# A never-entered branch with idle instructions at the head of three engine programs

## The chip, the cores and the metric
The kernel runs on one core of one Trainium2 chip. The metric is the device time of one execution in microseconds (us). Three runs of the kernel before gave 166.06, 166.07 and 166.12 us, a median of 166.07 us.

## The reference
The input is `x` with shape (32, 512, 1024) in float32, all values positive, 64 MiB in all. The output is one sum for each row of 1024 values.

```python
def reference(x: np.ndarray) -> np.ndarray:
    return np.sum(1.0 / x, axis=-1).astype(np.float32)
```

So each of the 16384 rows is inverted element by element and summed.

## The kernel before
The 16384 rows lie on 128 partitions, 128 rows on each. A unit of work is one row on every partition, a 128x1024 tile of 512 KB. There are 127 whole units, and the last row is cut into two pieces of 512 columns. Units are loaded into a ring of 46 rows in on-chip memory (`ring`), and their sums are collected in `sums`, 128x128.

Nothing is scheduled by the framework. The string `PLAN` (lines 41 to 59) lists the steps by hand, and the loop at line 161 sends each token to its engine in that order. The letters that matter here are these.

- `D` loads units through SyncE's (SP's) queue, line 170. The first loads are 2, 12, 12, 9 and 11 units; the last ones are single units and the two halves. A load into ring rows that are in use waits for the engines that still read them.
- `A` on ScalarE (ACT), line 178, replaces a unit by the reciprocal of its square root. Squared and summed, that gives the sum of reciprocals.
- `Z` on ACT, line 187, squares and sums in one pass. In the trace each `Z` is two instructions, an ACTIVATE and a read of the accumulator.
- `G` on GpSimd (POOL), line 280, squares; `T` on VectorE (DVE), line 283, sums what POOL squared; `Q` on DVE, line 240, squares and sums at once; `B` on DVE, line 255, takes statistics from which squares are summed later (`K`, `M`).
- For the pair units, `P` on POOL (line 194) multiplies the two halves of a row, `U` on TensorE (PE, line 201) adds the halves, `L` and `E` on ACT (line 211) take the reciprocal square root of the product and square it, and `R` on DVE (line 220) multiplies and sums.
- Stores of parts of `sums` go through SP, line 156: six of them late in the plan and the last one at the end.

At the head, line 70 loads ACT's function table, and `make_identity` at line 90 has POOL fill a 128x128 identity matrix (masks.py:197 and 199) that PE needs for `U`. Ahead of the plan's loop, lines 159 and 160 issue 13 instructions on POOL that do nothing (`EARLY = 13`, line 21). Each engine has a program of its own, a straight line of instructions from head to end; it meets the others only at semaphores. As built, ACT's program for this kernel has 133 instructions (156 with the second half of each `Z` or accumulating step), DVE's 174, POOL's 101, SP's 68 and PE's 48 before its matrix instructions are split. An instruction is 64 bytes long.

Of the kernel before, what the change touches and what calls it, by code (L numbers as in the profile page):

```python
# [11 lines left out]
def kernel(  # L12
# [5 lines left out]
    nc = tc.nc  # L18
    f32 = mybir.dt.float32
    P = 128  # L20
    EARLY = 13
    D = 1024
    H = D // 2
    F = 128
# [67 lines left out]
    def parse(tok):  # L92
        body, _, b = tok[1:].partition("@")
        r, _, n = body.partition("+")
        return tok[0], int(r), int(n or 1), int(b or 0)
# [58 lines left out]
    def store(lo, hi):  # L154
        a, at = divmod(lo, HALF)
        nc.sync.dma_start(out=out_v[a, :, at : at + hi - lo], in_=sums[:, lo:hi])

    with tc.manual_schedule():
        for _ in range(EARLY):
            nc.gpsimd.nop(hint="idle", nofuse=True)  # L160
        for op, u, n, b in (parse(tok) for tok in PLAN):
            if op == "D":
                n, u = u, loaded
                while n:
# [10 lines left out]
                    u, n = u + m, n - m  # L175
# [83 lines left out]
            elif op in "KM":  # L259
                lo, step, n = STATS[u]  # L260
                i = stat_rows.index(lo)
                part = stats[:, i : i + n]
                if op == "K":
# [4 lines left out]
                    engine = "ACT"  # L268
                else:
# [6 lines left out]
                    engine = "DVE"  # L276
# [47 lines left out]
```

## Time and profile before
| what | value |
|---|---|
| median of three runs | 166.07 us (166.06 to 166.12) |
| span of the profiled execution | 164.2 us |
| ACT busy | 145.7 us, 89% of the span |
| DVE busy | 115.9 us, 71% |
| POOL busy | 108.8 us, 66% |
| PE busy | 38.2 us, 23% |
| read from HBM | 67.11 MB, 409 GB/s over the span |
| packets of the queue of data | 4608, 96.3% of 16 DMA engines' span |
| packets of the queue of instructions | 3 |

The profiled execution's own span is 164.2 us, from the first to the last instruction of the program on the core; the runs' times also hold about 1.8 us that lie outside of it. Times inside the span are counted from its start. Busy time does not count instructions that only wait, branch or set registers. The data of a load is cut into one packet per partition and load, and the 16 DMA engines carry the packets side by side. A load has landed when the last of the 16 has brought its part.

### The profile page before, as it was taken

The page shows a single profiled execution, that of the slowest core. Times are in us where ns is not written, and L with a number is a line of the kernel's source. Part 1 is how long each engine was busy: PE and PEld are TensorE (multiplying, and loading weights), DVE is VectorE, ACT ScalarE, POOL GpSimd, SP SyncE. Part 2 cuts the span into 40 slices and gives each one's busy share as a digit, 9 for nine tenths or more (in the row PEclk, how much of TensorE's full clock was granted, in tenths as well). Part 3 has the DMA queues.
Part 4 walks back from the last instruction along what each step waited for, and adds up shares of the span by engine and source line. Part 5 has one row for each costly group of instructions (what it writes and reads, how often), then busy time and mean ns, then how long its engine had stood idle before and what let it go on. Part 6 is the DMA issues. An engine that isn't in the chain of part 4 may idle for free.

```text
span 164.2 us, 640 instructions
## 1 busy us (share of the span) xinstructions
PE 38.2 (23%) x68; PEld 14.4 (9%) x68; DVE 115.9 (71%) x147; ACT 145.7 (89%) x148; POOL 108.8 (66%) x56
## 2 busy tenths in 40 slices
PE   0000000000000000053000000065908198699700
PEld 0000000000000000020000000032302033234200
DVE  0000003559927039999999999999698969999894
ACT  3600199999999999999999999999999999999994
POOL 1000069998999999999507979999926195477300
PEclk9999999999999999999999999999975859999985
DMA  5999899899989899999998998999999999999970
GB/s 188 463 539 407 383 395 563 383 431 431 463 351 527 351 479 409 391 455 431 391 503 383 431 463 381 455 407 441 419 425 467 414 419 422 421 411 417 408 249 2
DMA packets 4611, 67.20 MB, mean 409 GB/s; under 512 B 1408, under 2 KB 1408, under 8 KB 2176
## 3 DMA queue, kind: packets, MB, share of 16 engines
q1 hardware_dynamic: 4608, 67.18, 96.3%
q14 instruction: 3, 0.02, 0.0%
HBM read 67.11 MB, written 0.07 MB: 409 GB/s over the span
## 4 chain that ended last, share of the span: by engine, by line
ACT 63%; DMA 26%; DVE 6%; issue 2%; POOL 2%; SPq 0%; DVEq 0%; POOLq 0%
ACT ring L178 47%; DMA ring<-in_x_dram 26%; ACT ring L187 10%; ACT prod L211 6%; DVE ring L240 2%; DVE stats L255 2%; POOL prod L194 2%; DVE prod L220 1%; DVE sums L283 0%; SPq L170 0%; ACT stats L265 0%; DVE sums L240 0%; DVE sums L220 0%; DVEq L240 0%; POOLq L194 0%
## 5 line engine op out<-in xcount | busy, mean ns | idle before, releaser
L178 ACT ACTIVATE ring<-ring 128x1024 f32<-128x1024 f32 (+4 forms) x65 | 104.1, 1658 | 15.2 <-DMA ring<-in_x_dram 15.1
L280 POOL TENSOR_TENSOR ring<-ring 128x1024 f32<-128x1024 f32 (+2 forms) x33 | 85.9, 2634 | 29.9 <-ACT ring L178 29.9
L283 DVE TENSOR_REDUCE sums<-ring 128x1 f32<-128x1024 f32 (+4 forms) x27 | 53.3, 1999 | 42.2 <-POOL ring L280 42.1
L201 PE MATMUL ps<-ring,ident 128*128 128x512 f32 x68 | 38.2, 712 | 117.2 <-DMA ring<-in_x_dram 115.9
L255 DVE BATCH_NORM_STATS2 stats<-ring 128x6 f32<-128x512 f32 x58 | 36.5, 679 | 3.1 <-ACT ring L178 3.1
L194 POOL TENSOR_TENSOR prod<-ring 128x512 f32<-128x512 f32 x17 | 22.5, 1339 | 15.0 <-DMA ring<-in_x_dram 10.8
L201 PEld LDWEIGHTS ps<-ring,ident 128*128 128x128 f32 x68 | 14.4, 224 | 140.2 <-POOL ring L280 71.6
L187 ACT ACTIVATE ring<-ring 128x1024 f32<-128x1024 f32 x23 | 23.9, 1041 | 0.0
L211 ACT ACTIVATE prod<-prod 128x512 f32<-128x512 f32 x34 | 19.8, 615 | 0.2
L240 DVE CUSTOM_DVE_ANT_0 ring<-ring 128x1024 f32<-128x1024 f32 (+1 forms) x12 | 17.6, 1480 | 0.5 <-ACT ring L178 0.4
L220 DVE CUSTOM_DVE_ANT_0 prod<-prod,ps 128x512 f32<-128x512 f32 x17 | 11.1, 676 | 0.1
L187 ACT ACTIVATION_READ_ACCUMULATOR ring<-ring 128x1 f32 x23 | 4.3, 187 | 0.0
L70 ACT ACT_TABLE_LOAD x1 | 1.3, 1283 | 0.7 <-PEq L308 0.7
L220 DVE DVE_READ_ACCUMULATOR2_ANT sums<- 128x1 f32 x17 | 1.4, 81 | 0.0
L240 DVE DVE_READ_ACCUMULATOR2_ANT sums<- 128x1 f32 x13 | 1.0, 81 | 0.0
L240 DVE CUSTOM_DVE_ANT_0 ring<-ring,sums 128x512 f32<-128x512 f32 x1 | 0.8, 752 | 0.1
masks.py:199 POOL TENSOR_SCALAR_AFFINE_SELECT ident<-ident 128x128 f32<-128x128 f32 x1 | 0.3, 293 | 0.5 <-POOL ident masks.py:197 0.5
L265 ACT ACTIVATE stats<-stats 128x44 f32<-128x44 f32 (+1 forms) x2 | 0.5, 272 | 0.0
L270 DVE TENSOR_REDUCE sums<-stats 128x11 f32<-128x88 f32 (+1 forms) x2 | 0.5, 264 | 0.0
masks.py:197 POOL MEMSET ident<- 128x128 f32 x1 | 0.2, 205 | 0.3 <-POOLq L308 0.3
L308 POOL MEMSET const-float32-0.0<- 128x1 f32 x1 | 0.1, 99 | 0.2 <-issue 0.2
L308 POOL MEMSET const-bfloat16-1.0<- 128x1 bf16 x1 | 0.1, 102 | 0.0
(2 smaller groups left out, 0.2 us busy)
## 6 DMA issues: line engine op xcount, KB each, us to landing
ring<-in_x_dram SPq DMA_DIRECT2D x2, 6144.0 KB, 25.8
ring<-in_x_dram SPq DMA_DIRECT2D x3, 4096.0 KB, 26.0
ring<-in_x_dram SPq DMA_DIRECT2D x3, 3072.0 KB, 26.3
ring<-in_x_dram SPq DMA_DIRECT2D x1, 5632.0 KB, 55.9
ring<-in_x_dram SPq DMA_DIRECT2D x1, 5120.0 KB, 32.4
ring<-in_x_dram SPq DMA_DIRECT2D x1, 4608.0 KB, 43.3
ring<-in_x_dram SPq DMA_DIRECT2D x4, 1024.0 KB, 37.8
ring<-in_x_dram SPq DMA_DIRECT2D x1, 3584.0 KB, 24.4
```

Of the source, the lines that this page charges most:

```text
L70: nc.scalar.add_instruction(mybir.InstLoadActFuncSet(name=nc.get_next_instruction_name(), act_func_set_id=act_sets.index("abs_reciprocal_s ...
L178: inst = nc.scalar.activation(out=area(u, n), in_=area(u, n), func=Arsqrt if op == "A" else Square, scale=FIT if op == "A" else 1.0,)
L187: inst = nc.scalar.activation(out=area(u), in_=area(u), func=Square, accum_out=sums[:, r : r + 1])
L194: inst = nc.gpsimd.tensor_tensor(out=prod[:, b], in0=ring[:, r, :H], in1=ring[:, r, H:], op=mult)
L201: inst = nc.tensor.matmul(ps[:, b], lhsT=ident, rhs=ring[:, r, h * H : (h + 1) * H], start=h == 0, stop=h == 1,)
L211: inst = nc.scalar.activation(out=pair, in_=pair, func=Arsqrt if op == "L" else Square, scale=S * FIT if op == "L" else 1.0,)
L220: inst = nc.vector.tensor_tensor_reduce(out=pair, in0=pair, in1=ps[:, bank[u]], scale=S, scalar=0.0, op0=mult, op1=add, accum_out=sums[:, ...
L240: inst = nc.vector.tensor_tensor_reduce(out=row, in0=row, in1=row, scale=1.0, scalar=total if r in summed else 0.0, op0=mult, op1=add, acc ...
L255: inst = nc.vector.bn_stats(out=stats[:, i, h], in_=ring[:, u % R, h * H : (h + 1) * H])
L265: inst = nc.scalar.activation(out=mean, in_=mean, func=Square, scale=float(H // 2) ** 0.5)
L280: inst = nc.gpsimd.tensor_tensor(out=row, in0=row, in1=row, op=mult)
L283: inst = nc.vector.tensor_reduce(out=sums[:, u : u + n], in_=area(u, n), axis=mybir.AxisListType.X, op=add,)
```

## The change
Lines 159 and 160 go, and with them POOL's 13 idle instructions. In their place, ahead of the plan, a register is set to zero on ACT, DVE and POOL, and a branch compares it with zero. The body of the branch, which is never entered, holds 60 idle instructions on POOL, 44 on ACT and 48 on DVE. Everything else of the program stands as it was.

```diff
-    EARLY = 13
+    EARLY = ((nc.gpsimd, 60), (nc.scalar, 44), (nc.vector, 48))
...
+    skippers = [mybir.EngineType.Activation, mybir.EngineType.DVE, mybir.EngineType.Pool]
+    never = nc.alloc_registers("never", engines=skippers)
+    nc.regs_mov(never, 0)
+    with tc.If(nc.snap(never, engines=skippers) != 0):
+        for engine, n in EARLY:
+            for _ in range(n):
+                engine.nop(hint="idle", nofuse=True)
     with tc.manual_schedule():
-        for _ in range(EARLY):
-            nc.gpsimd.nop(hint="idle", nofuse=True)
         for op, u, n, b in (parse(tok) for tok in PLAN):
```

As built, each of the three programs gains two register moves, the compare-and-branch, the idle instructions and one unconditional branch behind them. That is 48 instructions more ahead of ACT's first ACTIVATE and 52 more ahead of DVE's first reduction. POOL's identity now stands ahead of the branch, and with a repeated one-instruction configuration behind the branch and the 13 idle ones gone its first TENSOR_TENSOR stands 52 further down. SP and PE get one unconditional branch each, to the instruction that follows; SP's stands between the first load and the second. All waits, semaphore counts and tiles of the other instructions are the same in both programs.

## The prediction
> **What bounds the kernel now.** I read the page's busy times and queues first.
>
> ```profile
> span 164.2 us, 640 instructions
> ...
> PE 38.2 (23%) x68; PEld 14.4 (9%) x68; DVE 115.9 (71%) x147; ACT 145.7 (89%) x148; POOL 108.8 (66%) x56
> ...
> q1 hardware_dynamic: 4608, 67.18, 96.3%
> q14 instruction: 3, 0.02, 0.0%
> ```
>
> Two things are nearly full: ACT (145.7 of 164.2 us) and the 16 DMA engines (96.3%). The last row is small but decides this case: three packets of 0.02 MB in all, about 8 KB each, brought instructions while the kernel ran. Next, ACT alone: its first instructions by time, and its busy time in stretches (the columns behind the stretch are its length and ACT's busy time).
>
> ```profile
> 0.74 1.28 ACT L70 ACT_TABLE_LOAD   x1 [0.74 <-PEq L308]
> 5.48 1.91 ACT L178 ACTIVATE ring<-ring 128x2048 f32<-128x2048 f32 x1 [3.46 <-DMA ring<-in_x_dram]
> ...
> 19.97 2.00 ACT L178 ACTIVATE ring<-ring 128x1024 f32<-128x1024 f32 x2 [11.40 <-DMA ring<-in_x_dram]
> ```
> ```profile
> 19.96:100.45 80.49, 80.48 (x66) 1.00 0.99 429
> 100.45:100.67 0.22, 0.00 (x0) 1.00 0.71 223
> 100.67:123.78 23.11, 23.10 (x26) 0.95 1.00 429
> 123.78:123.88 0.10, 0.00 (x0) 0.50 0.00 0
> 123.88:161.90 38.02, 37.82 (x52) 0.86 0.93 383
> ```
>
> ACT waits 11.40 us for the second load, starts at 19.97, and is then busy to 161.90 with two holes, at 100.45 (0.22 us) and 123.78 (0.10 us). At both its next step is the first use of a load. Back-to-back ACT steps overlap by about 0.10 us, so the holes cost about 0.32 and 0.20, together **0.52 us**. So the end is set by when the second load lands, by ACT's 142 us behind it, and by any load that lands late.
>
> **Where the instruction packets fall.** The DMA view, cut to three short windows, finds one packet in each: 65.5 to 66.0, 99.9 to 100.3, and 111.9 to 112.2 us.
>
> ```profile
> q14 instruction: 1, 0.01, 3.9%
> ```
> ```profile
> q14 instruction: 1, 0.01, 5.1%
> ```
> ```profile
> q14 instruction: 1, 0.01, 6.4%
> ```
>
> The share is of 16 engines in the window: 3.9% of 16 x 0.5 us is 0.31 us; the others give 0.33 and 0.31. The data packet behind it suffers as well. At 64.2 to 64.4 seven packets of 40 KB start; at 66.0 to 66.5, behind the first instruction packet, one starts.
>
> ```profile
> q1 hardware_dynamic: 7, 0.29, 331.7%
> ```
> ```profile
> q1 hardware_dynamic: 1, 0.04, 23.7%
> ```
>
> The seven took 331.7% of 3.2 us, 1.52 us each; the one took 23.7% of 8 us, 1.90 us. So one instruction packet sets one DMA engine back by up to 0.31 + 0.38 = **0.69 us**, and since a load lands with its slowest engine, every later load lands later by about that. Holes of 0.32 and 0.20 us at first uses, behind the first packet and behind all three, fit this.
>
> Whose packets are they? 8 KB at 64 bytes is 128 instructions. ACT's program (156) and DVE's (174) are longer than that, so each must pass an 8 KB border at least once. Counted by stretch (PE, PEld, DVE, ACT, POOL in this order):
>
> ```profile
> 0.00:65.80 65.80, 0.00 (x0) 0.00 (x0) 23.96 (x10) 50.17 (x42) 43.79 (x22) 1.00 0.99 424
> 65.80:100.20 34.40, 3.75 (x4) 1.17 (x4) 34.17 (x38) 34.40 (x28) 26.50 (x11) 1.00 0.98 422
> 100.20:112.10 11.90, 4.02 (x6) 1.89 (x7) 11.79 (x13) 11.67 (x11) 11.90 (x6) 1.00 1.01 430
> 112.10:146.00 33.90, 21.43 (x40) 7.74 (x38) 30.78 (x55) 33.70 (x47) 20.30 (x15) 0.85 1.00 427
> 146.00:164.20 18.20, 9.04 (x20) 3.58 (x20) 15.24 (x35) 15.79 (x25) 6.33 (x5) 0.85 0.73 285
> ```
>
> ACT has started 42 instructions at 65.8, DVE 48 at 100.2, POOL 39 at 112.1 (to which its 13 idle ones and some ten that only wait are to be added). The skipped stretch covers ACT's places 7 to 51, DVE's 6 to 54 and POOL's 17 to 77, so I take the first packet as ACT's, the second as DVE's, the third as POOL's: all three borders then lie inside the skipped stretch. ACT has no idle time at 65.8, so the packet is read ahead, not awaited.
>
> **The change, part by part.**
>
> ```profile
> 0.73 0.20 POOL masks.py:197 MEMSET ident<- 128x128 f32 x1 [0.29 <-POOLq L308]
> 1.45 0.29 POOL masks.py:199 TENSOR_SCALAR_AFFINE_SELECT ident<-ident 128x128 f32<-128x128 f32 x1 [0.51 <-POOL ident masks.py:197]
> 22.05 10.57 POOL L280 TENSOR_TENSOR ring<-ring 128x3072 f32<-128x3072 f32 x2 [20.31 <-ACT ring L178]
> ```
> ```profile
> 0.74 2.54 SPq L170 DMA_DIRECT2D ring<-in_x_dram  x5
> ```
> ```profile
> 27.39 3.41 DVE L283 TENSOR_REDUCE sums<-ring 128x1 f32<-128x1024 f32 x2 [27.39 <-POOL ring L280]
> ```
>
> *POOL's 13 idle instructions* lie between 0.73 and 1.45, so they are worth at most 0.72 us, and POOL waits from then to 22.05: gain nothing. *Two moves and the branch* on three engines aren't in this trace. Above, they cannot cost much more than that 0.72 us for 13 idle instructions and more; below, nothing. ACT waits till 5.48, POOL till 22.05, DVE till 27.39, so both ends give 0. Without that cover ACT would pay up to 0.72. *SP's extra branch* delays the second of five issues, which come every 0.5 us and are done at 3.28, while the first load runs till 5.48: 0. [...]
>
> *The three packets* move to the head: entering the next block at about 1 us asks for the one behind it. What follows has four terms.
>
> (a) The 0.52 us of holes can go, since at 100.45 and 123.78 no engine has been set back in mid-run.
>
> (b) At the head the packets may meet the first data. No data packet starts before 1.75 us, and the stretches there (the last columns are the DMA share and GB/s) show:
>
> ```profile
> 1.00:1.75 0.75, 0.00 (x0) 0.00 (x0) 0.00 (x0) 0.75 (x1) 0.29 (x1) 1.00 0.00 0
> 1.75:2.25 0.50, 0.00 (x0) 0.00 (x0) 0.00 (x0) 0.27 (x1) 0.00 (x0) 1.00 1.56 262
> 2.25:4.50 2.25, 0.00 (x0) 0.00 (x0) 0.00 (x0) 0.00 (x0) 0.00 (x0) 1.00 0.90 353
> ```
>
> From SP's first issue (0.74) to the first data is 1.0 us; an instruction packet asked for at 1 us and as slow would come at about 2.0, on top of the first rows. If quicker it is done before them. So the setback is between 0 and 0.69 us, and it moves the second load's landing and ACT's start at 19.97. I take 0.2: it is asked for hardly later than the data, and the engines run below their later rate in that stretch anyway (353 against 429 GB/s), so part of it hides. By 123.9 ACT is ahead by 0.52 - 0.2 = 0.32 us.
>
> (c) The shift brings new borders into the run. ACT's next one is 128 places on, and 48 places come earlier: its instruction 42 + 128 - 48 = 122, 26 from the end. DVE's is 76 instructions behind its 48th, about 124 less the dozen places that only wait, some 35 from the end. By the last row above (x35, x25) both are at about 146 us. POOL has none. So two of the three packets come again, in the tail, and if they use the same DMA engines as before the last loads land as late as now, plus (b).
>
> (d) In the tail the loads are barely ahead of ACT. The load issued at 109.78 and the last one, issued at 148.39, each with its size and us to landing, then ACT's steps that use them:
>
> ```profile
> 109.78 0.33 SPq L170 DMA_DIRECT2D ring<-in_x_dram  x1
> ```
> ```profile
> ring<-in_x_dram SPq DMA_DIRECT2D x1, 1024.0 KB, 38.5
> ```
> ```profile
> 148.39 0.33 SPq L170 DMA_DIRECT2D ring<-in_x_dram  x1
> ```
> ```profile
> ring<-in_x_dram SPq DMA_DIRECT2D x1, 256.0 KB, 11.5
> ```
> ```profile
> 148.56 1.04 ACT L178 ACTIVATE ring<-ring 128x1024 f32<-128x1024 f32 x1
> ```
> ```profile
> 158.74 2.08 ACT L178 ACTIVATE ring<-ring 128x1024 f32<-128x1024 f32 x3
> ```
>
> They land at 148.3 and 159.9; ACT uses them at 148.56 and, as the third of three (0.95 + 0.52 behind 158.74), at 160.2. So ACT can be at most about 0.25 us earlier there before it waits again.
>
> The sum: ACT's gain of 0.32 is cut in the tail to 0.25 - 0.2 = **0.05 us**. The profiled span is 164.24 us and would become 164.2; the runs' median is 1.83 us above it, so 166.07 - 0.05 gives 166.0.
>
> **The rivals.** *Faster: the packets come early and the tail stays free.* If they are done before 1.75 us, (b) is 0; if the tail's packets are absent or fall on engines that have slack, (d) doesn't bind, and the whole 0.52 us is won: 165.55. For it: no data runs before 1.75. Against it: the 8 KB packets, which put the next border at 146. [...]
>
> *Slower: head collision.* If all 0.69 us of (b) is paid, (c) and (d) leave 0.25 - 0.69 = -0.44: 166.5. It decides from 0.58 us on (0.25 + 0.33). For it: three engines are hit, and the slowest counts. Against it: the slow first rows that hide a part.
>
> *Slower: the jump breaks reading ahead.* If a taken branch doesn't start the read of the block behind, ACT and DVE must wait at 146 us for a packet: 1.0 us from asking to the first data, as SP's at the head, plus 0.31, less little: ACT is on the path there, so +1.2: 167.3. [...] Nothing in this trace shows a long jump.
>
> *It doesn't do what it says.* If the borders lie elsewhere, packets only move to other times: 166.05.
>
> **How the numbers follow.** A measurement of this kernel tells about 0.2%, 0.33 us, from no change. Forecast (165.75 to 166.4) 0.49; faster rival 0.25; head collision 0.12; broken reading 0.10; no effect 0.04. Faster 0.25, same 0.49 + 0.04 = 0.53, slower 0.22. The range goes from the faster rival to the collision with a little beyond, 165.5 to 166.6; left out are the broken reading and the edges.
>
> **What would show it.** Right: no instruction packet between 5 and 140 us, none or three near 1 to 2 us, two near 146; the hole at 100.45 gone; ACT's long run starting at 20.0 to 20.3. The faster rival shows ACT starting at 19.97 and no packet in the tail. The collision shows ACT starting at 20.4 or later. Broken reading shows an ACT hole of about 1 us near 146 with no data load as its releaser. Packets in mid-run would make the mapping wrong.

## The result and the profile after
The changed kernel takes 166.81 us (166.75 to 166.99, three runs) against 166.07 us. The ratio is 1.0044, 95% interval 1.0024 to 1.0064: slower by 0.74 us, beyond the predicted range. The profiled execution's span went from 164.2 to 165.0 us. First the page of the changed kernel: span, busy times, queues and the chain that ended last by engine.

```profile
span 165.0 us, 638 instructions
...
PE 39.7 (24%) x68; PEld 14.8 (9%) x68; DVE 116.1 (70%) x147; ACT 145.8 (88%) x148; POOL 108.7 (66%) x56
...
q1 hardware_dynamic: 4608, 67.18, 95.8%
q14 instruction: 5, 0.04, 0.1%
...
ACT 64%; DMA 31%; DVE 2%; issue 1%; SPq 0%; DVEq 0%
```

ACT has the same work (145.8 against 145.7 us). The instruction queue has five packets in the span instead of three, and the chain of waits spends 31% on data loads where it spent 26%. The DMA view cut to four short windows of the changed kernel shows where the five lie: 5.0 to 5.2, 6.6 to 6.8, 149.5 to 149.8 and 151.9 to 152.1 us.

```profile
q14 instruction: 1, 0.01, 9.7%
```
```profile
q14 instruction: 2, 0.02, 19.3%
```
```profile
q14 instruction: 1, 0.01, 6.5%
```
```profile
q14 instruction: 1, 0.01, 10.2%
```

Between 7 and 149 us there are none. What the three at the head cost shows in the data packets that start where they end, at 5.38, 6.98 and 7.02 us. The first line is a data packet of the same size at 6.58 that follows no instruction packet, the other three are these; the windows are 20, 15, 15 and 12 ns long.

```profile
q1 hardware_dynamic: 1, 0.05, 567.2%
```
```profile
q1 hardware_dynamic: 1, 0.05, 849.6%
```
```profile
q1 hardware_dynamic: 1, 0.05, 942.1%
```
```profile
q1 hardware_dynamic: 1, 0.05, 1232.3%
```

The undisturbed packet took 567.2% of 16 x 0.02 us, which is 1.82 us; in the same way the three took 2.04, 2.26 and 2.37. Now ACT by time and, below, by stretches (length, busy time and count, granted clock, DMA share, GB/s):

```profile
5.60 1.91 ACT L183 ACTIVATE ring<-ring 128x2048 f32<-128x2048 f32 x1 [3.58 <-DMA ring<-in_x_dram]
...
20.77 2.00 ACT L183 ACTIVATE ring<-ring 128x1024 f32<-128x1024 f32 x2 [12.08 <-DMA ring<-in_x_dram]
```
```profile
20.76:100.90 80.14, 80.13 (x65) 0.86 1.00 431
100.90:124.10 23.20, 23.20 (x28) 0.72 1.00 429
124.10:154.17 30.07, 30.01 (x43) 0.79 1.00 424
154.17:154.35 0.18, 0.01 (x2) 1.00 1.04 410
154.35:155.40 1.05, 1.05 (x1) 1.00 1.02 406
155.40:155.63 0.23, 0.01 (x2) 1.00 1.08 427
155.63:162.70 7.07, 7.01 (x10) 0.83 0.51 173
```
```profile
154.35 1.06 ACT L183 ACTIVATE ring<-ring 128x1024 f32<-128x1024 f32 x1 [0.17 <-DMA ring<-in_x_dram]
155.63 1.06 ACT L183 ACTIVATE ring<-ring 128x1024 f32<-128x1024 f32 x1 [0.22 <-DMA ring<-in_x_dram]
```

The reader is to see three things. ACT starts its long run 0.80 us later (20.77 against 19.97). Both holes of before, at 100.45 and 123.78, are gone. New holes stand in the tail, at first uses of loads. Matched instruction by instruction in the two traces, ACT is late by 0.80 us from 20 to 100 us, by 0.46 at 102, 0.23 at 124, 0.07 at 150.3, and then by about 0.78 from 155 to the end. So the late start was won back almost wholly, and the tail lost it again. Had the first been all, the time would have been nearly that of before.

The last load, in SP's row and the DMA view of the changed kernel:

```profile
148.46 0.33 SPq L175 DMA_DIRECT2D ring<-in_x_dram  x1
```
```profile
ring<-in_x_dram SPq DMA_DIRECT2D x1, 256.0 KB, 12.3
```

It lands at 160.8 us, 0.9 later than before (148.39 + 11.5); the loads that land behind 153 us are all 0.9 to 1.0 us later.

### The profile page after: what moved, and what is told of

Read it like the earlier page. It is cut to its first block, busy times and chain, and to the rows that moved or that the text cites. A ratio compares the mean times of both kernels' runs of the same rounds, so it can differ in the third digit from the quotient of the medians.

```text
span 165.0 us, 638 instructions
## 1 busy us (share of the span) xinstructions
PE 39.7 (24%) x68; PEld 14.8 (9%) x68; DVE 116.1 (70%) x147; ACT 145.8 (88%) x148; POOL 108.7 (66%) x56
## 4 chain that ended last, share of the span: by engine, by line
ACT 64%; DMA 31%; DVE 2%; issue 1%; SPq 0%; DVEq 0%
ACT ring L183 48%; DMA ring<-in_x_dram 31%; ACT ring L192 13%; ACT prod L216 3%; DVE ring L245 2%; DVE prod L225 0%; SPq L175 0%; ACT stats L270 0%; DVE sums L245 0%; DVEq L245 0%; DVEq L324 0%; DVE sums L225 0%
## 5 line engine op out<-in xcount | busy, mean ns | idle before, releaser
L206 PE MATMUL ps<-ring,ident 128*128 128x512 f32 x68 | 39.7, 735 | 116.7 <-DMA ring<-in_x_dram 115.3
```

Of the source, the lines that this page charges most:

```text
L206: inst = nc.tensor.matmul(ps[:, b], lhsT=ident, rhs=ring[:, r, h * H : (h + 1) * H], start=h == 0, stop=h == 1,)
```

## The experiments
All were compared with the kernel before on the same chip, where its median was 166.06 to 166.08 us. The first question is whether it is the branch or the packets.

**e1, the branch without a shift.**
```diff
-    EARLY = ((nc.gpsimd, 60), (nc.scalar, 44), (nc.vector, 48))
+    EARLY = ((nc.gpsimd, 8), (nc.scalar, 1), (nc.vector, 1))
```


> The same branch on the three engines, but with a body of 1 idle instruction on ScalarE and VectorE and 8 on GpSimd, so that the places of the instructions move by 5, 5 and 0 only and the three instruction packets stay in mid-run. Theory A (the time is lost by instruction packets that meet the load stream at the head and again in the tail): packets near 60, 95 and 112 us, none before 20 us and none behind 140 us, ScalarE starts its second load at 19.9 to 20.1 us, time 166.0 to 166.2. Rival B (the branch, its register moves or the second configuration of GpSimd cost it): ScalarE's start or the end moves by 0.7 us, time 166.7 to 166.9.

Measured: 166.10 us, ratio 1.0003 (0.9994 to 1.0011). The packets came at 64, 93 and 112 us. Branch, register moves and POOL's repeated configuration cost nothing that can be seen. Rival B falls.

**e2, the shift without a branch.**
```diff
-    EARLY = 13
+    EARLY = ((nc.gpsimd, 65), (nc.scalar, 48), (nc.vector, 52))
...
-        for _ in range(EARLY):
-            nc.gpsimd.nop(hint="idle", nofuse=True)
+        for engine, n in EARLY:
+            for _ in range(n):
+                engine.nop(hint="idle", nofuse=True)
```


> No branch: the idle instructions are run at the head, 48 on ScalarE, 52 on VectorE and 65 on GpSimd, so that every later instruction has the same place as in the changed kernel. Theory A: packets at 5 to 10 us and two near 150 us as in the changed kernel, ScalarE's second start at 20.5 to 20.9 us, time 166.6 to 167.0. Rival B: no branch, so 166.0 to 166.2.

Measured: 166.80 us, ratio 1.0046 (1.0033 to 1.0059), packets at 6.6, 6.7, 8.4, 149.0 and 151.8 us, ACT's second start at 20.66. So the places of the instructions decide, not how the idle ones are passed, and rival B falls here too.

**e3, the same shift in mid-run.** It tells the head from the tail.
```diff
+        idle = {"A40+4": (nc.scalar, 48), "T33+3": (nc.vector, 52), "G30+3": (nc.gpsimd, 52)}
+        last = ""
-        for op, u, n, b in (parse(tok) for tok in PLAN):
+        for tok in PLAN:
+            if last in idle:
+                engine, many = idle[last]
+                for _ in range(many):
+                    engine.nop(hint="idle", nofuse=True)
+            last = tok
+            op, u, n, b = parse(tok)
```


> No branch: 48, 52 and 52 idle instructions are run on ScalarE, VectorE and GpSimd near 40 to 55 us, behind long steps; GpSimd keeps its 13 at the head. The first packets then come near 40 to 55 us, the second two near 150 us, none at the head. Theory A1 (the tail's second packets on engines already set back decide the end): ScalarE's second start stays at 19.9 to 20.1 us, a wait of 0.3 to 1 us comes near 100 us, the last loads land 0.5 to 1.0 us later than before, time 166.4 to 166.9. Rival A2 (the late start at the head decides, the tail does nothing): time 166.0 to 166.2.

Measured: 166.73 us, ratio 1.0048 (1.0035 to 1.0061). Two of e3's rows of ACT by time, its second start and the tail:

```profile
20.01 4.66 ACT L186 ACTIVATE ring<-ring 128x1024 f32<-128x1024 f32 x3 [11.40 <-DMA ring<-in_x_dram]
```
```profile
155.51 1.06 ACT L186 ACTIVATE ring<-ring 128x1024 f32<-128x1024 f32 x1 [0.23 <-DMA ring<-in_x_dram]
```

The start is where it was before, and the time is nearly that of the change. The late start is not needed; A2 falls. The second packets came at 148.9 and 151.8 us, as expected. One expectation missed: the first packets came at 59, 64 and 75 us, since ScalarE's and VectorE's idle instructions ran at 59 to 61 and 69 to 72 us, later than I had read from the plan, and no longer wait came at 100 us.

**e4, e5, e6, one engine at a time** (the same branch, on one engine's list; e5 and e6 keep the 13 idle instructions).
```diff
+    EARLY = ((nc.gpsimd, 60),)
+    skippers = [mybir.EngineType.Pool]
```


> The branch and its 60 idle instructions on GpSimd alone; ScalarE's and VectorE's programs keep their places. Theory A1: one packet at 5 to 7 us, two in mid-run at 65 and 100 us, none in the tail; ScalarE's second start is 0.3 to 0.8 us later, and the tail lands as before (each DMA engine is hit once), so time 165.9 to 166.3. Rival A2 (the late start at the head decides): 166.4 to 166.8.

> The branch and its 44 idle instructions on ScalarE alone; GpSimd keeps its 13 run ones, VectorE's program keeps its places. ScalarE's packets: one at 3 to 7 us, one at 149 to 150 us; VectorE's at 100 and GpSimd's at 112 us stay. Theory A1 (setbacks add up on the DMA engine that carries one program's packets, and the slowest engine's total by the tail decides): ScalarE's engine is hit twice, about 0.7 + 0.7 us, so the last loads land 0.3 to 0.6 us later than before and 166.2 to 166.6. Theory A3 (each packet only counts where it falls, nothing adds up): 166.0 to 166.15.

> The branch and its 48 idle instructions on VectorE alone; GpSimd keeps its 13 run ones, ScalarE's program keeps its places. VectorE's packets: one at 3 to 7 us, one at 151 to 152 us; ScalarE's at 65 and GpSimd's at 112 us stay. VectorE's packet cost its DMA engine the most in the kernel before (0.33 + 0.66 us), so by theory A1 the last loads land 0.6 to 1.0 us later than before and the time is that of the whole change, 166.5 to 166.9. Theory A3: 166.0 to 166.15.

Measured: e4 166.09 us, ratio 0.9999 (0.9990 to 1.0008), although ACT started at 20.43; e5 166.41, ratio 1.0014 (1.0004 to 1.0023); e6 166.80, ratio 1.0042 (1.0028 to 1.0055). Each engine's packets moved and the others' stayed, which also names them: ACT's is the one near 66 us, DVE's at 100, POOL's at 112. (One time missed: POOL's packet in e4 came at 3.4 us, not at 5 to 7.) POOL's move is free: e4 has no packet behind 100.5 us, since POOL's program ends before a second border. DVE's alone costs as much as the whole change; in e6 ACT meets the same two waits in the tail.

```profile
154.65 1.06 ACT L185 ACTIVATE ring<-ring 128x1024 f32<-128x1024 f32 x1 [0.28 <-DMA ring<-in_x_dram]
155.94 1.06 ACT L185 ACTIVATE ring<-ring 128x1024 f32<-128x1024 f32 x1 [0.23 <-DMA ring<-in_x_dram]
```

The costs of ACT's and DVE's moves, 0.33 and 0.72 us, would be 1.05 together, and the whole change costs 0.74: they do not add up, which fits that only the slowest DMA engine counts.

**e7, the 13 idle instructions away** (`EARLY = 0` in the kernel before).

> The part of the change that removes GpSimd's 13 run instructions, alone. GpSimd's border is passed 13 instructions later, so its packet comes near 130 us instead of 112; the other two stay at 65 and 100 us. All theories: each DMA engine is hit once, 166.0 to 166.2. If the 13 instructions cost time by themselves, it would be 0.3 us or more faster.

Measured: 166.39 us, ratio 1.0022 (1.0013 to 1.0032), above the range expected. POOL's row by time at 142 us in the kernel before, the same step in e7, and ACT's row in e7:

```profile
142.31 2.51 POOL L194 TENSOR_TENSOR prod<-ring 128x512 f32<-128x512 f32 x2 [2.40 <-DVE stats L255]
```
```profile
142.64 1.28 POOL L194 TENSOR_TENSOR prod<-ring 128x512 f32<-128x512 f32 x1 [2.75 <-DVE stats L255]
```
```profile
145.19 1.67 ACT L211 ACTIVATE prod<-prod 128x512 f32<-128x512 f32 x3 [0.47 <-POOL prod L194]
```

In the kernel before this POOL step started 0.10 us behind the DVE step that released it; in e7 it starts 0.45 us behind it, and ACT waits 0.47 us for its product. The packet follows at 145.8 us. So I take the extra 0.34 us as POOL's program passing the border, with nothing queued to cover it: the size is that of the gap in POOL's rows of idle instructions (e2 and e3, below), but no run moves this border by a few places to test it. The 13 instructions had kept it off this spot.

**e8, second packets earlier.**
```diff
+        idle = {"A56+6": (nc.scalar, 92), "T23+6": (nc.vector, 112)}
```
(in e3's loop)

> No branch: 92 idle instructions run on ScalarE behind A56+6 and 112 on VectorE behind T23+6, beside steps of 5 to 6 us that hide them; GpSimd keeps its 13. ScalarE's packets then come at 65 and near 110 us, VectorE's near 60 to 75 and near 110 us, GpSimd's at 112; none at the head, none in the tail. Theory A1 (setbacks add up and stay to the end): the last loads land 0.7 to 1.0 us later although no packet falls behind 120 us, 166.5 to 166.9. Theory A3 (a packet only counts in the tail): 166.0 to 166.2.

Measured: 167.03 us, ratio 1.0060 (1.0046 to 1.0074), just above the range expected. Packets at 67, 85, 112, 112 and 126 us (the last one later than expected) and none behind. In e8 ACT meets the late loads early:

```profile
116.09 2.76 ACT L186 ACTIVATE ring<-ring 128x3072 f32<-128x3072 f32 x1 [0.52 <-DMA ring<-in_x_dram]
```

And the delay stays: the loads that land behind 131 us are 0.95 to 1.0 us later than before, the last one at 160.7 us 0.83, long after the last packet. Each DMA engine ends its part of a load with a small packet of 4 bytes, its end mark. In a load that ends near 131 us, the 16 end marks show two engines 1.78 and 2.02 us behind the first; in the kernel before the worst there is 1.22. So setbacks add up on an engine, and A3 falls.

**e9, loads after the packets.**
```diff
     with tc.manual_schedule():
+        for _ in range(40):
+            nc.sync.nop(hint="idle", nofuse=True)
```


> The changed kernel with 40 idle instructions on SyncE ahead of its first load, so that the load stream starts 1.6 us later and the three head packets have time to come first. (SyncE's program is 40 longer, and may read one more block in mid-run, on an engine of its own.) Theory A1: the three packets come before the first data, which start near 3.4 us; no DMA engine is set back at the head, so ScalarE's second start is 1.6 to 1.8 us later than before (21.6 to 21.8 us), the last loads land 1.5 to 1.8 us later than before and not 2.6, time 167.3 to 167.7. If the setback came from something else than meeting the data, the start would be at 22.3 us and the time 168.1 to 168.6.

Measured: 167.50 us, ratio 1.0089 (1.0073 to 1.0104). The DMA view of e9 from 0 to 3.2 us holds no data packet, only:

```profile
q14 instruction: 3, 0.02, 2.0%
```
```profile
21.53 2.00 ACT L185 ACTIVATE ring<-ring 128x1024 f32<-128x1024 f32 x2 [11.41 <-DMA ring<-in_x_dram]
```

With the way free the packets come at 2.2 to 2.6 us. ACT's second start is 1.56 us later than before, about the 1.5 us by which the data start later (3.22 against 1.75), and the last loads 1.55. Without the meeting there is no setback at the head. Packets come again at 150.5 and 152.8 us (and one at 136.3, as allowed for SyncE), with lengthened data packets behind them, and yet the last loads are late by hardly more than the start of the data. So the tail's packets cost next to nothing where no engine had been set back at the head. Starting later isn't worth the delay.

**e10, no border passed twice.**
```diff
-    EARLY = ((nc.gpsimd, 60), (nc.scalar, 44), (nc.vector, 48))
+    EARLY = ((nc.gpsimd, 60), (nc.scalar, 30), (nc.vector, 12))
```


> The changed kernel with 30 instead of 44 idle instructions on ScalarE and 12 instead of 48 on VectorE, 60 on GpSimd. The stalls in the rows of idle instructions that were run put the borders at place 64 in ScalarE's and VectorE's programs and 69 in GpSimd's, and so the next at 192; now ScalarE's and VectorE's programs end at place 190. Theory A1: GpSimd's packet at 3 to 5 us, ScalarE's near 25 to 32 us, VectorE's near 85 to 92 us, none in the tail, each DMA engine hit once; ScalarE's second start 0.1 to 0.6 us later than before, the last loads land within 0.3 us of before, time 165.9 to 166.3. If the branch with all three skips costs whatever the borders: 166.6 to 166.9.

Measured: 166.22 us, ratio 1.0011 (1.0002 to 1.0020). In its span there are three packets, at 4.8, 24.7 and 92.0 us, and none in the tail; the span is that of before:

```profile
span 164.2 us, 638 instructions
```

So 0.6 of the 0.74 us go when 14 and 36 of the skipped instructions go. What is left, 0.16 us, lies outside of the span. Two instruction packets at 166.2 us of this trace, behind the span's end, suggest that ScalarE's and VectorE's next border is read there; that was not tried by itself. No kernel here beats the kernel before.

## Why the prediction was wrong
- **What bounds the kernel, and term (a).** Right in what bounds it and in the size: both holes, 0.52 us, went, and ACT won back 0.73 of its 0.80 us by 150.3. The reason given for (a) did not hold. The loads at whose first use the holes lay land no earlier, at 100.80 against 100.65 us and at 123.91 against 123.86, since the engines had been set back at the head. The holes went because ACT itself came later, so the size came out right for another reason.
- **Whose packets, and the second borders, term (c).** Right in whose packet is whose (e4 to e6), in that two come again in the tail (149.6 and 151.9 against the 146 expected), and that they hit engines already set back. Wrong in where the borders are. Where idle instructions are run across a border, the trace shows them 0.04 to 0.05 us apart with one gap: 0.34 us on ACT near place 64 (e3 and e8), 0.47 on DVE near the same place, 0.39 on POOL near place 69 (e2 and e3), and the packet 3 to 4 us behind each. So ACT's and DVE's borders lie about 12 and 9 places behind the skipped stretch, not in it; only POOL's lies in it. Nor does it take a program of over 128 instructions to pass a border, as I had argued for ACT and DVE: POOL's program of 101 passes one. It made little difference, since here a program is read ahead of what is executed: before, ACT's packet came when place 44 was being executed.
- **Term (b), the setback at the head. This step failed.** I had said "I take 0.2" of 0 to 0.69 us, because the packets would come hardly later than the data and hide in the slow first rows. They came 4 to 5.8 us behind the branches (0.89 to 1.11), at 5.07, 6.68 and 6.71, amid the full stream; with the way free they came within 1.5 us (e9). They cost 0.53, 0.76 and 0.86 us (0.31 us of its own each, and the 0.22, 0.45 and 0.55 us by which the data packet behind it took longer), and ACT's start moved by 0.80. The bound of 0.69 was too low as well: it was read off the first packet of before alone, while the second, DVE's, had cost 0.33 + 0.66 = 0.99 us.
- **Term (d), the sum.** Its form was right, and (b)'s size decided the sign. The margin of 0.25 us less the 1.0 us by which the loads behind 153 us landed late is -0.75; measured was -0.74. Of that 1.0 us the DMA engines' spread accounts for 0.86, which is the size of the costliest head packet: in the load that lands at 154.3 us the slowest engine is 2.05 us behind the first, before 1.19. The rest, by which the first engine too was later, is not explained.
- **Rivals.** The head collision was the case that happened (its price of 0.44 us too small by the same term), and what it cost was decided in the tail, not at the start (e3, e4). The faster rival fell. An instruction packet is 8 KB here (five are 0.04 MB), 128 instructions of 64 bytes, and the runs fit that: the first border is near place 64 (e3, e8), programs of 190 places passed no second one inside the span (e10), and programs of 204 and 226 (ACT's and DVE's in the change) pass one. The jump did not break the reading ahead: ACT has no hole without a data load near 149 us. But ACT's and DVE's jumps pass no border; POOL's alone does, and POOL waits for data long after it, so what a jump over a border costs a busy engine stays open.

## What to carry to other kernels
In these runs each border that a program passed, one near place 64 (69 on POOL) and the next 128 places on by the packets' size, fetched code while the kernel ran. Padding did not remove a fetch: it moved it and brought another one in at the end (five packets in the change, three before), so count the borders that each program passes from its first to its last instruction. With a load stream that was never idle, a DMA engine that was set back stayed behind (e8, 0.83 us at the last load); the last loads show the sum on the worst engine, wherever the fetches were. A delay at the head may be repaid by waits that vanish later, so follow how late the bounding engine is through the whole run before naming the cause.

## What the runs showed of the hardware
- One 8 KB instruction packet takes 0.31 to 0.34 us but sets its DMA engine back by 0.52 (e4, at 3.4 us) to 0.99 us where it meets the load stream. VectorE's cost 0.98 to 0.99 in the kernel before and in the tails of the change, e2, e3 and e6 alike, at the head of e6 0.85; why it costs more than ScalarE's 0.68 to 0.69 in the kernel before and in the tails of the change, e2 and e3 is open.
- Passing a border holds the engine's program for 0.30 to 0.42 us beyond an idle instruction's own time (e2, e3 and e8). In the kernel's time it showed only in e7, by the reading given there.
- A compare-and-branch took 0.045 us on ScalarE and GpSimd and 0.056 us on VectorE in the trace of the change.
